# A LoRA kernel on one Trainium2 core: all of x held in SBUF, loads ahead of stores, groups of four tiles

## The chip, the core and the metric

The kernel runs on one core of one Trainium2 chip. The core has a matmul engine (PE, whose weight loads are listed apart as PEld), a vector engine (DVE), a scalar engine (ACT), GpSimd (POOL) and a sync engine (SP), which run their own instruction streams and meet at semaphores, and 16 DMA engines that carry data between the chip's memory (HBM) and the on-chip memory (SBUF, 128 partitions). PE writes to PSUM, a second on-chip memory. The metric is device time in microseconds of one execution; lower is better.

## The reference

```python
batch, seq, d_model, r = 16, 512, 768, 16
x: (16, 512, 768) float32;  A: (768, 16);  B: (16, 768);  scale = 0.5

def reference(x, A, B, scale):
    lora = np.matmul(np.matmul(x, A), B)
    return (x + scale * lora).astype(np.float32)
```

8192 tokens of 768 numbers go in and out: 25.2 MB each way. The two matmuls are thin (rank 16).

## The kernel before

**Tiles.** 128 tokens make a tile, 64 tiles in all; in SBUF a tile takes 768 floats in each of the 128 partitions. `PARTS` cuts the tiles into blocks of 8, 8, 16, 16 and 16. In a block of S tiles each partition holds S tokens that follow each other in memory, so that a load or a store moves one long run for each partition. `x_all` has room for `ROOM` = 48 tiles; the last block uses the places of tiles 0 to 15 again. The sum is written over x in place and stored from there.

**Groups.** The compute goes by groups of `GROUP` = 8 tiles, `NG` = 8 groups. Each group takes these steps:

- `narrowed`: ACT casts the first four tiles of x to half precision into `xn`, POOL the other four.
- `turned`: DVE transposes `xn` in blocks of 32 x 32 words into `xt`. A word is a pair of half-precision numbers, so the pair stays together.
- `projected`: PE multiplies `xt` by the block-diagonal `w_bd` (made from A in the start-up) in 24 matmuls that add up in `y_ps`; the moving side has 32 columns for each tile of the group, 256 here.
- ACT scales the four quarters of `y_ps` into the block-diagonal `y_bd` (four `e.mul`).
- `raised(p)`: for each pair of tiles PE multiplies `y_bd` by `b_mm` (B, spread over the partitions) into one of two PSUM buffers `lora`, four matmuls for a pair.
- `summed(g, p)` on DVE adds `lora` to the pair of x tiles in place.

There is one `xn`, one `xt`, one `y_bd`, one `y_ps`. `s_taken` tells that PE has begun to read a group's `xt` (so `xn` may be written again), `s_y` that its projection is done, `s_lora` counts raised pairs, `s_free` gives a PSUM buffer back, `s_sum` counts the blocks whose sums are complete.

**Order.** It is written out by hand for each engine. DVE transposes group g+1 ahead of group g's four sums. PE runs a loop over the groups: raise two pairs, half of the next projection, raise two pairs, the other half. SP issues every transfer on one queue: loads 0 to 5 at the start (A and B between them), then, when two groups are summed, stores 0 and 1; it waits until store 0 has landed and issues load 6 into its place, the same with store 1 and load 7, and then issues stores 2 to 4 as their sums are done. The function `summed(k)` in SP's part waits for `s_sum` and then also gives PE the last PSUM buffer of that group.

**Start-up.** POOL clears buffers, makes the selection matrix `pick`, casts B and builds `w_bd` from the transposed A; PE spreads B with `pick`; ACT copies it to `b_mm`.

Of the kernel before, what the change touches and what calls it, by code (L numbers as in the profile page):

```python
# [10 lines left out]

PARTS = [8, 8, 16, 16, 16]


GROUP = 8

SUB = 4

# [8 lines left out]
def kernel(  # L29
# [28 lines left out]
    def ps(name, shape):  # L58
        return nc.alloc_psum_tensor(name, shape, fp32).ap()

    ROOM = sum(PARTS[:-1])
    x_all = sb("x_sb", [P, ROOM, D], fp32)

    a_rows = sb("a_rows", [P, 64 * R], fp32)
    a_t = sb("a_t", [P, 2, R, Q], fp32)
    w_one = sb("w_one", [Q, NC, 2, R], MM_DT)
    b_rows = sb("b_rows", [P, D], fp32)  # L70
    b_half = sb("b_half", [P, D], MM_DT)
    pick = sb("pick", [P, NQ, Q], MM_DT)
    w_bd = sb("w_bd", [P, NC, 2, P], MM_DT)
    b_mm = sb("b_mm", [P, D], MM_DT)
    xn = sb("xn", [P, GROUP, D], MM_DT)
    xt = sb("xt", [P, GROUP, D], MM_DT)
    y_bd = sb("y_bd", [P, GROUP, P], MM_DT)
    lora = [ps(f"lora_ps{i}", [P, 2, D]) for i in range(2)]
    y_ps = ps("ps_yt", [P, GROUP, Q])

    sems = []

# [20 lines left out]
    def tiles(t, n):  # L103
        return x_all[:, ds(t % ROOM, n), :]

    LOADS = [
        (0, 0, 2), (0, 2, 6), (1, 0, 8), (2, 0, 8), (2, 8, 8), (3, 0, 16), (4, 0, 8), (4, 8, 8)
    ]
    s_load = [sem(f"s_load{k}") for k in range(len(LOADS))]

# [4 lines left out]
    assert SETS * SET == NC  # L115
    s_a, s_b = sem("s_a"), sem("s_b")
    s_ready, s_brows, s_pick = sem("s_ready"), sem("s_brows"), sem("s_pick")
    s_w, s_bh, s_bp, s_bm = sem("s_w"), sem("s_bh"), sem("s_bp"), sem("s_bm")
    s_first, s_narrow, s_turned, s_taken = sem("s_first"), sem("s_narrow"), sem("s_turned"), sem("s_taken")
    s_y, s_spread, s_lora = sem("s_y"), sem("s_spread"), sem("s_lora")  # L120

    s_free = [sem(f"s_free{p}") for p in range(PAIRS)]
    s_out0, s_out1, s_raise = sem("s_out0"), sem("s_out1"), sem("s_raise")

    s_sum, s_out = sem("s_sum"), sem("s_out")

    MMS = 2 * NC
    STORES = [(0, 0, 8), (1, 0, 8), (2, 0, 16), (3, 0, 16), (4, 0, 16)]

    STORED = [where.index((i, s + n - 1)) // GROUP for i, s, n in STORES]  # L130

# [3 lines left out]
    def on_sync(e):  # L135
        def load(k):
            ld = LOADS[k]
            e.dma_start(out=held(*ld), in_=memory(x2, *ld)).then_inc(s_load[k], 16)  # L138

        def summed(k):  # L140
            e.wait_ge(s_sum, k + 1)
            if STORED[k] + 1 < NG:

                e.sem_inc(s_free[PAIRS - 1], 1)

        def store(k, done):
            st = STORES[k]
            e.dma_start(out=memory(out2, *st), in_=held(*st)).then_inc(done, 16)

        load(0)  # L150
        load(1)
        e.wait_ge(s_ready, 1)
        blocks = A.rearrange("(c e) r -> c (e r)", e=64)
        for c in range(SETS):
            e.dma_start(
                out=a_rows[c : SET * SET : SET, :], in_=blocks[ds(c * SET, SET), :]
            ).then_inc(s_a, 16)
        e.wait_ge(s_brows, 1)
        e.dma_start(out=b_rows[0 : R * APART : APART, :], in_=B).then_inc(s_b, 16)
        for k in range(2, len(LOADS) - 2):  # L160
            load(k)

        for p in range(2, PAIRS):
            e.sem_inc(s_free[p], 1)
        summed(0)
        summed(1)


        e.wait_ge(s_lora, 2 * PAIRS + 2)
        store(0, s_out0)  # L170
        store(1, s_out1)
        e.wait_ge(s_out0, 16)
        load(len(LOADS) - 2)
        e.wait_ge(s_out1, 16)
        load(len(LOADS) - 1)
        for k in range(2, len(STORES)):
            summed(k)
            if k == 2:


                e.wait_ge(s_raise, 6)
            store(k, s_out)

    here = set()

    def narrowed(e, copy, g, first, n=SUB):
        t = g * GROUP + first
        for k in dict.fromkeys(load_of(t + k) for k in range(n)):
            if (e, k) not in here:
                here.add((e, k))  # L190
                e.wait_ge(s_load[k], 16)
        if g:
            e.wait_ge(s_taken, g)
        ins = copy(out=xn[:, ds(first, n), :], in_=tiles(t, n))  # L194

        ins.then_inc(s_narrow if g else s_first if first else s_a, 1)

    def on_gpsimd(e):
        e.memset(a_rows[0:Q], 0.0).then_inc(s_ready, 1)  # L199
        e.memset(b_rows, 0.0).then_inc(s_brows, 1)  # L200
        e.memset(pick, 0.0).then_inc(s_pick, 1)
        e.memset(w_bd.rearrange("p c k m -> p (c k m)").bitcast(fp32), 0.0)  # L202
        e.memset(y_bd.rearrange("p s m -> p (s m)").bitcast(fp32), 0.0).then_inc(s_ready, 1)  # L203
        e.wait_ge(s_pick, 1)
        e.affine_select(  # L205
            out=pick, in_=pick, compare_op=mybir.AluOpType.not_equal, fill=1.0, base=0,
            pattern=[[0, NQ], [-APART, Q]], channel_multiplier=1,
        ).then_inc(s_pick, 1)
        narrowed(e, e.tensor_copy, 0, 0, SUB // 2)
        e.wait_ge(s_pick, 2)  # L210
        e.wait_ge(s_b, 16)
        e.tensor_copy(out=b_half, in_=b_rows).then_inc(s_bh, 1)  # L212
# [6 lines left out]
        for b in range(NQ):  # L219
# [4 lines left out]
        for g in range(1, NG):  # L224
            narrowed(e, e.tensor_copy, g, SUB)

    def on_scalar(e):
        narrowed(e, e.copy, 0, SUB // 2, SUB // 2)
        narrowed(e, e.copy, 0, SUB)
        e.wait_ge(s_bp, 1)  # L230
        e.copy(out=b_mm, in_=lora[0][:, 0, :]).then_inc(s_bm, 1)  # L231
        for g in range(NG):
            if g + 1 < NG:
                narrowed(e, e.copy, g + 1, 0)
            e.wait_ge(s_y, g + 1)
            for b in range(NQ):
                q = ds(b * Q, Q)
                last = e.mul(out=y_bd[q, :, q], in_=y_ps[q, :, :], mul=sc)  # L238
            last.then_inc(s_spread, 1)

    def on_vector(e):
# [6 lines left out]
        def turned(first, n):  # L248
            ts = [v[:, ds(first, n), :].bitcast(fp32) for v in (xt, xn)]
            return e.transpose(out=ts[0], in_=ts[1])  # L250

        def summed(g, p):
            xs = tiles(g * GROUP + 2 * p, 2)
            e.wait_ge(s_lora, g * PAIRS + p + 1)
            ins = e.tensor_tensor(out=xs, in0=xs, in1=lora[p % 2], op=mybir.AluOpType.add)  # L255
            if p + 1 == PAIRS and g in STORED:
                ins.then_inc(s_sum, 1)
            elif g + 1 < NG or p + 2 < PAIRS:
                ins.then_inc(s_free[p], 1)

        for h in range(2):
            e.wait_ge(s_first, h + 1)
            ins = turned(h * SUB, SUB)
        ins.then_inc(s_turned, 1)
        for g in range(NG):
            if g + 1 < NG:
                e.wait_ge(s_y, g + 1)
                e.wait_ge(s_narrow, 2 * (g + 1))  # L268
                turned(0, GROUP).then_inc(s_turned, 1)
            for p in range(PAIRS):  # L270
                summed(g, p)

    def on_tensor(e):


        xv = xt.rearrange("p s (c j k) -> p s c j k", c=NC, k=2)

        def projected(first, last):
            for m in range(first, last):
                c, k = divmod(m, 2)  # L280
                mm = e.matmul(  # L281
                    y_ps, w_bd[:, c, k, :], xv[:, :, c, :, k],
                    start=(m == 0), stop=(m == MMS - 1),
                )
                if m == 0:
                    mm.then_inc(s_turned, -1)
# [6 lines left out]
        def raised(p):  # L293
            if p == 0:
                e.wait_ge(s_spread, 1)
            free = s_free[(p + 2) % PAIRS]
            e.wait_ge(free, 1)
            t = lora[p % 2]
            mms = []
            for k in range(2):  # L300
                for n0, w in ((0, 512), (512, 256)) if k == 0 else ((0, 256), (256, 512)):
                    mms.append(e.matmul(  # L302
                        t[:, k, ds(n0, w)], y_bd[:, 2 * p + k, :], b_mm[:, ds(n0, w)],
                        start=True, stop=True,
                    ))
            if p == 0:
                mms[0].then_inc(s_raise, 1)
# [9 lines left out]
                b_half[:, ds(n0, w)], start=True, stop=True,  # L317
            )
        last.then_inc(s_bp, 1)
        e.wait_ge(s_w, 1 + NQ)  # L320
        e.wait_ge(s_turned, 1)
        projected(0, MMS)
        e.wait_ge(s_bm, 1)
        with e.Fori(0, NG - 1):
            raised(0)
            raised(1)
            e.wait_ge(s_turned, 1)
            projected(0, MMS // 2)
            raised(2)
            raised(3)  # L330
            projected(MMS // 2, MMS)
        for p in range(PAIRS):
            raised(p)

    on_sync(nc.sync)
    on_gpsimd(nc.gpsimd)
# [6 lines left out]

    nc.gpsimd.wait_ge(s_sum, len(STORED))
    nc.gpsimd.sem_clear(range(nums[0], s_sum.num))
    nc.gpsimd.wait_ge(s_out, (len(STORES) - 2) * 16)
    nc.gpsimd.sem_clear(range(s_sum.num, s_out.num + 1))
    section.close()

# [34 lines left out]
```

## Time and profile before

| | |
|---|---|
| median of 3 runs | 123.55 us (123.46 to 123.61) |
| profiled execution: span, first to last instruction | 121.9 us |
| HBM read, written | 25.26 MB, 25.17 MB |
| mean rate over the span | 414 GB/s |
| DVE, PE, ACT, POOL busy | 81.7, 50.5, 37.4, 28.4 us |

The profile shows one execution. A row of a group reads: line, engine, operation, tile written <- tiles read, shapes, count | busy us in total, mean ns of one | idle time of that engine just before, and what ended it. A row in order of time begins with its start and duration in us; in square brackets stands how long the engine had been idle, and what released it. SPq is SP's sequencer, which issues DMAs. A stretch gives its start and end, its length, the busy time of each engine with the number of instructions, PEclk (the clock granted to PE, 1.00 is full speed), the busy share of the 16 DMA engines and the rate; a packet counts where it starts. The digits over 40 slices are tenths. Busy time of an engine is not yet a bound: which wait ends last decides.

### The profile page before, as it was taken

How to read it: one execution, taken by the hardware profiler on the slowest of the kernel's cores; microseconds unless marked ns; L12 is line 12 of the kernel's file. 1: busy time of each engine (PE TensorE's matmuls, PEld its weight loads, DVE VectorE, ACT ScalarE, POOL GpSimd, SP SyncE). 2: the span in 40 equal slices, each digit the busy share in tenths (PEclk: the TensorE clock that was granted, in tenths of full speed). 3: DMA queues.
4: the chain of work that ended last, by engine and by line, in shares of the span. 5: the costliest groups of instructions: out<-in, count | busy, mean ns of one | idle time of the engine just before them, and what ended most of it. 6: DMA issues, size and time to landing. Idle time of an engine off the chain costs nothing.

```text
span 121.9 us, 885 instructions
## 1 busy us (share of the span) xinstructions
PE 50.5 (41%) x322; PEld 29.3 (24%) x322; DVE 81.7 (67%) x42; ACT 37.4 (31%) x43; POOL 28.4 (23%) x24
## 2 busy tenths in 40 slices
PE   0000239487457457647756714774674320000000
PEld 0000026244233233424424402442442110000000
DVE  0003850799999999999999959999995991000000
ACT  4003929444426402917230093643004000000000
POOL 7732638044026002607100090630000000000000
PEclk9999999999999999999999999999999985555555
DMA  3999999999997996999989999998998999899890
GB/s 67 421 429 429 443 443 403 451 435 419 476 516 339 435 516 298 460 403 443 443 363 460 427 427 468 451 484 387 419 500 387 403 516 403 371 516 419 355 516 0
DMA packets 1928, 50.43 MB, mean 414 GB/s; under 512 B 236, under 2 KB 236, under 8 KB 392
## 3 DMA queue, kind: packets, MB, share of 16 engines
q1 hardware_dynamic: 1928, 50.43, 96.8%
HBM read 25.26 MB, written 25.17 MB: 414 GB/s over the span
## 4 chain that ended last, share of the span: by engine, by line
DVE 33%; DMA 29%; PE 9%; ACT 6%; POOL 2%; issue 2%; SPq 0%; DVEq 0%
DVE x_sb L255 21%; DMA x_sb<-in_x_dram 20%; DVE xt L250 12%; DMA out_dram<-x_sb 9%; PE ps_yt L281 6%; ACT xn L194 3%; PE lora_ps L302 3%; ACT y_bd L238 2%; POOL xn L194 2%; SPq L138 0%; SPq L379 0%; DVEq L268 0%; SPq L133 0%
## 5 line engine op out<-in xcount | busy, mean ns | idle before, releaser
L255 DVE TENSOR_TENSOR x_sb<-x_sb,lora_ps 128x1536 f32<-128x1536 f32 x32 | 53.7, 1735 | 1.4 <-PE lora_ps L302 1.4
L302 PE MATMUL lora_ps<-b_mm,y_bd 128*128 128x512 f16 (+1 forms) x128 | 25.1, 328 | 23.7 <-ACT y_bd L238 15.3
L194 ACT CAST xn<-x_sb 128x3072 f16<-128x3072 f32 (+1 forms) x9 | 23.4, 2609 | 37.2 <-DMA x_sb<-in_x_dram 28.0
L250 DVE STREAM_TRANSPOSE xt<-xn 128x3072 f32<-128x3072 f32 (+1 forms) x9 | 27.0, 3005 | 6.7 <-PE ps_yt L281 4.9
L194 POOL CAST xn<-x_sb 128x3072 f16<-128x3072 f32 (+1 forms) x8 | 20.7, 2588 | 45.3 <-DMA x_sb<-in_x_dram 28.6
L281 PE MATMUL ps_yt<-xt,w_bd 128*128 128x256 f16 x192 | 25.7, 285 | 11.9 <-DVE xt L250 11.9
L281 PEld LDWEIGHTS ps_yt<-xt,w_bd 128*128 128x128 f16 x192 | 18.7, 100 | 19.6 <-issue 15.0
L302 PEld LDWEIGHTS lora_ps<-b_mm,y_bd 128*128 128x128 f16 x128 | 10.5, 97 | 36.8 <-ACT y_bd L238 17.5
L238 ACT ACTIVATE y_bd<-ps_yt 32x256 f16<-32x256 f32 x32 | 12.0, 374 | 17.7 <-PE ps_yt L281 17.4
L243 DVE STREAM_TRANSPOSE a_t<-a_rows 32x1024 f32<-32x1024 f32 x1 | 1.9, 1945 | 11.2 <-DMA a_rows<-in_A_dram 11.2
L315 PE MATMUL lora_ps<-b_half,pick 128*128 128x512 f16 (+1 forms) x2 | 0.8, 500 | 12.5 <-POOL b_half L212 12.5
L315 PEld LDWEIGHTS lora_ps<-b_half,pick 128*128 128x128 f16 x2 | 0.1, 105 | 12.5 <-issue 12.5
L220 POOL COPY w_bd<-w_one 32x384 f16<-32x384 f16 x4 | 2.0, 501 | 0.2
L212 POOL CAST b_half<-b_rows 128x768 f16<-128x768 f32 x1 | 0.8, 830 | 4.5 <-DMA b_rows<-in_B_dram 4.5
L194 ACT ACT_TABLE_LOAD x1 | 1.3, 1283 | 0.9 <-SPq L133 0.9
L202 POOL MEMSET w_bd<- 128x1536 f32 x1 | 1.4, 1372 | 0.0
L199 POOL MEMSET a_rows<- 32x1024 f32 x1 | 0.9, 941 | 0.5 <-SPq L133 0.5
L214 POOL CAST w_one<-a_t 32x384 f16<-32x384 f32 x1 | 0.8, 847 | 0.9 <-DVE a_t L243 0.9
L231 ACT CAST b_mm<-lora_ps 128x768 f16<-128x768 f32 x1 | 0.8, 798 | 0.0
L200 POOL MEMSET b_rows<- 128x768 f32 x1 | 0.7, 727 | 0.0
L203 POOL MEMSET y_bd<- 128x512 f32 x1 | 0.5, 514 | 0.0
L205 POOL TENSOR_SCALAR_AFFINE_SELECT pick<-pick 128x128 f16<-128x128 f16 x1 | 0.3, 300 | 0.0
(5 smaller groups left out, 0.6 us busy)
## 6 DMA issues: line engine op xcount, KB each, us to landing
out_dram<-x_sb SPq DMA_DIRECT2D x3, 6144.0 KB, 20.0
x_sb<-in_x_dram SPq DMA_DIRECT2D x5, 3072.0 KB, 14.8
x_sb<-in_x_dram SPq DMA_DIRECT2D x1, 6144.0 KB, 41.9
out_dram<-x_sb SPq DMA_DIRECT2D x2, 3072.0 KB, 14.9
x_sb<-in_x_dram SPq DMA_DIRECT2D x1, 2304.0 KB, 9.7
x_sb<-in_x_dram SPq DMA_DIRECT2D x1, 768.0 KB, 4.5
a_rows<-in_A_dram SPq DMA_DIRECT2D x3, 16.0 KB
b_rows<-in_B_dram SPq DMA_DIRECT2D x1, 48.0 KB, 7.4
```

The source lines that it names most:

```text
L194: ins = copy(out=xn[:, ds(first, n), :], in_=tiles(t, n))
L199: e.memset(a_rows[0:Q], 0.0).then_inc(s_ready, 1)
L202: e.memset(w_bd.rearrange("p c k m -> p (c k m)").bitcast(fp32), 0.0)
L212: e.tensor_copy(out=b_half, in_=b_rows).then_inc(s_bh, 1)
L220: e.tensor_copy(out=w_bd[ds(b * Q, Q), :, :, ds(b * Q, R)], in_=w_one).then_inc(s_w, 1)
L238: last = e.mul(out=y_bd[q, :, q], in_=y_ps[q, :, :], mul=sc)
L243: e.transpose(out=a_t[0:Q].rearrange("i k r c -> i (k r) c"), in_=a_rows[0:Q].rearrange("c (i k r) -> c (k r) i", k=2, r=R),).then_inc(s_r ...
L250: return e.transpose(out=ts[0], in_=ts[1])
L255: ins = e.tensor_tensor(out=xs, in0=xs, in1=lora[p % 2], op=mybir.AluOpType.add)
L281: mm = e.matmul(y_ps, w_bd[:, c, k, :], xv[:, :, c, :, k], start=(m == 0), stop=(m == MMS - 1),)
L302: mms.append(e.matmul(t[:, k, ds(n0, w)], y_bd[:, 2 * p + k, :], b_mm[:, ds(n0, w)], start=True, stop=True,))
L315: last = e.matmul(lora[0][:, 0, ds(n0, w)], pick.rearrange("p b r -> p (b r)"), b_half[:, ds(n0, w)], start=True, stop=True,)
```

## The change

- `x_all` has room for all 64 tiles; the blocks are 8, 16, 16, 12 and 12. There are still eight loads and five stores: loads of 2, 6, 8, 8, 16, 12, 10 and 2 tiles, stores of whole blocks.
- SP issues loads 0 to 5 at the start, load 6 after the first raised pair, load 7 after the projection of group 7, then waits for load 6 to land and issues stores 0 and 1, and stores 2 to 4 as their sums are done.
- A group has 4 tiles, 16 groups. A projection's matmuls have 128 columns, a group has two pairs. `y_bd`, `y_ps` and the semaphores `s_turned` and `s_free` are doubled and go by even and odd groups. PE projects two groups ahead, in one piece after the raising of a group; DVE transposes group g+2 ahead of group g's two sums.
- The start-up's scratch (`a_rows`, `a_t`, `b_rows`, `b_half`, `pick`, `w_one`) and group 1's `xn` and `xt` lie in the part of `x_all` that load 6 fills.
- There is no `xt` of its own any more. Groups 0 and 2 to 7 are turned into the place of the last two tiles (which load 7 fills), groups 8 to 10 in place in `xn`, groups 11 to 15 into the place of tiles 0 and 1, after store 0 has landed. While a group is turned in place, the next cast waits for its projection (`s_y`) and not only for `s_taken`.
- DVE instead of POOL writes the last of the four copies of `w_bd`.
- PE's loop becomes two loops (three and two rounds of two groups) with groups written out between and behind them.

```diff
-PARTS = [8, 8, 16, 16, 16]
-GROUP = 8
-SUB = 4
+PARTS = [8, 16, 16, 12, 12]
+GROUP = 4
+SUB = 2
+PLACE = range(8, 11)
...
-    ROOM = sum(PARTS[:-1])
+    ROOM = sum(PARTS)
...
-    xt = sb("xt", [P, GROUP, D], MM_DT)
-    y_bd = sb("y_bd", [P, GROUP, P], MM_DT)
+    y_bd = sb("y_bd", [P, 2, GROUP, P], MM_DT)
-    y_ps = ps("ps_yt", [P, GROUP, Q])
+    y_ps = [ps(f"ps_yt{i}", [P, GROUP, Q]) for i in range(2)]
+    late = x_all[:, ds(ROOM - PARTS[-1], PARTS[-1]), :].rearrange("p s d -> p (s d)")
...
+    xt_a, xt_c = turned_in(ROOM - SUB), turned_in(0)
+    def narrow_of(g):
+        return xn_1 if g == 1 else xn
+    def turn_of(g):
+        return xt_1 if g == 1 else xt_a if g < PLACE[0] else xn if g in PLACE else xt_c
...
     LOADS = [
-        (0, 0, 2), (0, 2, 6), (1, 0, 8), (2, 0, 8), (2, 8, 8), (3, 0, 16), (4, 0, 8), (4, 8, 8)
+        (0, 0, 2), (0, 2, 6), (1, 0, 8), (1, 8, 8), (2, 0, 16), (3, 0, 12), (4, 0, 10), (4, 10, 2)
     ]
...
-    STORES = [(0, 0, 8), (1, 0, 8), (2, 0, 16), (3, 0, 16), (4, 0, 16)]
+    STORES = [(i, 0, S) for i, S in enumerate(PARTS)]
...
-        for p in range(2, PAIRS):
-            e.sem_inc(s_free[p], 1)
+        for p in range(PAIRS):
+            e.sem_inc(s_free[1][p], 1)
+        e.wait_ge(s_lora, 1)
+        load(len(LOADS) - 2)
         summed(0)
         summed(1)
-        e.wait_ge(s_lora, 2 * PAIRS + 2)
+        e.wait_ge(s_y, PLACE[0])
+        load(len(LOADS) - 1)
+        e.wait_ge(s_load[len(LOADS) - 2], 16)
         store(0, s_out0)
-        store(1, s_out1)
-        e.wait_ge(s_out0, 16)
-        load(len(LOADS) - 2)
-        e.wait_ge(s_out1, 16)
-        load(len(LOADS) - 1)
+        store(1, s_out)
         for k in range(2, len(STORES)):
             summed(k)
-            if k == 2:
-                e.wait_ge(s_raise, 6)
             store(k, s_out)
...
-        if g:
-            e.wait_ge(s_taken, g)
+        if g - 1 in PLACE:
+            e.wait_ge(s_y, g)
+        elif g > 1:
+            e.wait_ge(s_taken, g if g > 2 else 1)
...
         for g in range(NG):
-            if g + 1 < NG:
-                e.wait_ge(s_y, g + 1)
+            if g + 2 < NG:
+                if g + 2 == PLACE[-1] + 1:
+                    e.wait_ge(s_out0, 16)
+                elif g + 2 not in PLACE:
+                    e.wait_ge(s_y, g + 2 if g else 1)
                 e.wait_ge(s_narrow, 2 * (g + 1))
-                turned(0, GROUP).then_inc(s_turned, 1)
+                turned(g + 2)
             for p in range(PAIRS):
                 summed(g, p)
...
-        with e.Fori(0, NG - 1):
-            raised(0)
-            raised(1)
-            e.wait_ge(s_turned, 1)
-            projected(0, MMS // 2)
-            raised(2)
-            raised(3)
-            projected(MMS // 2, MMS)
-        for p in range(PAIRS):
-            raised(p)
+        def step(g):
+            for p in range(PAIRS):
+                raised(g % 2, p)
+            if g + 2 < NG:
+                projected(g % 2, turn_of(g + 2))
```

More of the change, by code (lines that the diff above doesn't have):

```diff
@@ L59, in ps @@
         return nc.alloc_psum_tensor(name, shape, fp32).ap()
-    ROOM = sum(PARTS[:-1])
+    ROOM = sum(PARTS)
     x_all = sb("x_sb", [P, ROOM, D], fp32)
[L67 to L72, printed above, removed]
     w_bd = sb("w_bd", [P, NC, 2, P], MM_DT)
@@ L75, with lent, turned_in @@
     xn = sb("xn", [P, GROUP, D], MM_DT)
-    xt = sb("xt", [P, GROUP, D], MM_DT)
-    y_bd = sb("y_bd", [P, GROUP, P], MM_DT)
+    y_bd = sb("y_bd", [P, 2, GROUP, P], MM_DT)
     lora = [ps(f"lora_ps{i}", [P, 2, D]) for i in range(2)]
-    y_ps = ps("ps_yt", [P, GROUP, Q])
+    y_ps = [ps(f"ps_yt{i}", [P, GROUP, Q]) for i in range(2)]
+    late = x_all[:, ds(ROOM - PARTS[-1], PARTS[-1]), :].rearrange("p s d -> p (s d)")
+    taken = [0]
+    def lent(n, dtype=fp32):
+        n = n if dtype is fp32 else n // 2
+        taken[0], first = taken[0] + n, taken[0]
+        assert taken[0] <= (PARTS[-1] - SUB) * D
+        v = late[:, ds(first, n)]
+        return v if dtype is fp32 else v.bitcast(dtype)
+    a_rows = lent(64 * R)
+    a_t = lent(2 * R * Q).rearrange("p (k r c) -> p k r c", k=2, r=R)
+    b_rows = lent(D)
+    b_half = lent(D, MM_DT)
+    pick = lent(P, MM_DT).rearrange("p (b r) -> p b r", b=NQ)
+    w_one = lent(NC * 2 * R, MM_DT)[0:Q].rearrange("i (c k r) -> i c k r", c=NC, k=2)
+    xn_1 = lent(GROUP * D, MM_DT).rearrange("p (s d) -> p s d", s=GROUP)
+    xt_1 = lent(GROUP * D, MM_DT).rearrange("p (s d) -> p s d", s=GROUP)
+    def turned_in(t):
+        v = x_all[:, ds(t, SUB), :].rearrange("p s d -> p (s d)").bitcast(MM_DT)
+        return v.rearrange("p (s d) -> p s d", s=GROUP)
+    xt_a, xt_c = turned_in(ROOM - SUB), turned_in(0)
[3 more added lines that the diff above has]
+        return xt_1 if g == 1 else xt_a if g < PLACE[0] else xn if g in PLACE else xt_c
     sems = []
@@ L117 @@
     s_ready, s_brows, s_pick = sem("s_ready"), sem("s_brows"), sem("s_pick")
+    s_wv = sem("s_wv")
     s_w, s_bh, s_bp, s_bm = sem("s_w"), sem("s_bh"), sem("s_bp"), sem("s_bm")
-    s_first, s_narrow, s_turned, s_taken = sem("s_first"), sem("s_narrow"), sem("s_turned"), sem("s_taken")
+    s_first, s_narrow, s_taken = sem("s_first"), sem("s_narrow"), sem("s_taken")
+    s_turned = [sem(f"s_turned{h}") for h in range(2)]
     s_y, s_spread, s_lora = sem("s_y"), sem("s_spread"), sem("s_lora")
-    s_free = [sem(f"s_free{p}") for p in range(PAIRS)]
-    s_out0, s_out1, s_raise = sem("s_out0"), sem("s_out1"), sem("s_raise")
+    s_free = [[sem(f"s_free{h}_{p}") for p in range(PAIRS)] for h in range(2)]
+    s_out0 = sem("s_out0")
     s_sum, s_out = sem("s_sum"), sem("s_out")
     MMS = 2 * NC
-    STORES = [(0, 0, 8), (1, 0, 8), (2, 0, 16), (3, 0, 16), (4, 0, 16)]
+    STORES = [(i, 0, S) for i, S in enumerate(PARTS)]
     STORED = [where.index((i, s + n - 1)) // GROUP for i, s, n in STORES]
@@ L142, in summed @@
             if STORED[k] + 1 < NG:
-                e.sem_inc(s_free[PAIRS - 1], 1)
+                e.sem_inc(s_free[STORED[k] % 2][PAIRS - 1], 1)
         def store(k, done):
@@ L191, in narrowed @@
                 e.wait_ge(s_load[k], 16)
-        if g:
-            e.wait_ge(s_taken, g)
-        ins = copy(out=xn[:, ds(first, n), :], in_=tiles(t, n))
-        ins.then_inc(s_narrow if g else s_first if first else s_a, 1)
+        if g - 1 in PLACE:
+            e.wait_ge(s_y, g)
+        elif g > 1:
+            e.wait_ge(s_taken, g if g > 2 else 1)
+        ins = copy(out=narrow_of(g)[:, ds(first, n), :], in_=tiles(t, n))
+        ins.then_inc(s_narrow if g > 1 else s_first if g or first else s_a, 1)
     def on_gpsimd(e):
@@ L202, in on_gpsimd @@
         e.memset(w_bd.rearrange("p c k m -> p (c k m)").bitcast(fp32), 0.0)
-        e.memset(y_bd.rearrange("p s m -> p (s m)").bitcast(fp32), 0.0).then_inc(s_ready, 1)
+        e.memset(y_bd.rearrange("p h s m -> p (h s m)").bitcast(fp32), 0.0).then_inc(s_ready, 1)
         e.wait_ge(s_pick, 1)
@@ L208, in on_gpsimd @@
         ).then_inc(s_pick, 1)
-        narrowed(e, e.tensor_copy, 0, 0, SUB // 2)
+        narrowed(e, e.tensor_copy, 0, 0)
         e.wait_ge(s_pick, 2)
@@ L218, in on_gpsimd @@
         e.wait_ge(s_w, 1)
-        for b in range(NQ):
+        for b in range(NQ - 1):
             e.tensor_copy(
@@ L223, in on_gpsimd @@
             e.wait_ge(s_w, b + 2)
-        for g in range(1, NG):
+        for g in range(2, NG):
             narrowed(e, e.tensor_copy, g, SUB)
     def on_scalar(e):
-        narrowed(e, e.copy, 0, SUB // 2, SUB // 2)
         narrowed(e, e.copy, 0, SUB)
+        narrowed(e, e.copy, 1, 0, GROUP)
         e.wait_ge(s_bp, 1)
         e.copy(out=b_mm, in_=lora[0][:, 0, :]).then_inc(s_bm, 1)
+        narrowed(e, e.copy, 2, 0)
         for g in range(NG):
-            if g + 1 < NG:
-                narrowed(e, e.copy, g + 1, 0)
             e.wait_ge(s_y, g + 1)
@@ L237, in on_scalar @@
                 q = ds(b * Q, Q)
-                last = e.mul(out=y_bd[q, :, q], in_=y_ps[q, :, :], mul=sc)
+                last = e.mul(out=y_bd[q, g % 2, :, q], in_=y_ps[g % 2][q, :, :], mul=sc)
             last.then_inc(s_spread, 1)
+            if 1 <= g < NG - 2:
+                narrowed(e, e.copy, g + 2, 0)
     def on_vector(e):
@@ L246, in on_vector, with turned @@
         ).then_inc(s_ready, 1)
-        def turned(first, n):
-            ts = [v[:, ds(first, n), :].bitcast(fp32) for v in (xt, xn)]
-            return e.transpose(out=ts[0], in_=ts[1])
+        def turned(g):
+            ts = [v.bitcast(fp32) for v in (turn_of(g), narrow_of(g))]
+            e.transpose(out=ts[0], in_=ts[1]).then_inc(s_turned[g % 2], 1)
         def summed(g, p):
@@ L257, in summed @@
                 ins.then_inc(s_sum, 1)
[L258 to L264, printed above, removed]
-        for g in range(NG):
-            if g + 1 < NG:
-                e.wait_ge(s_y, g + 1)
+            elif g + 1 < NG:
+                ins.then_inc(s_free[g % 2][p], 1)
+        for g in range(2):
+            e.wait_ge(s_first, g + 1)
+            turned(g)
+            if g == 0:
+                b = NQ - 1
+                e.wait_ge(s_w, 1)
+                e.tensor_copy(
+                    out=w_bd[ds(b * Q, Q), :, :, ds(b * Q, R)], in_=w_one
+                ).then_inc(s_wv, 1)
+        for g in range(NG):
+            if g + 2 < NG:
[3 more added lines that the diff above has]
+                    e.wait_ge(s_y, g + 2 if g else 1)
                 e.wait_ge(s_narrow, 2 * (g + 1))
-                turned(0, GROUP).then_inc(s_turned, 1)
+                turned(g + 2)
             for p in range(PAIRS):
@@ L273, in on_tensor, with projected @@
     def on_tensor(e):
-        xv = xt.rearrange("p s (c j k) -> p s c j k", c=NC, k=2)
-        def projected(first, last):
-            for m in range(first, last):
+        def projected(h, xt):
+            xv = xt.rearrange("p s (c j k) -> p s c j k", c=NC, k=2)
+            e.wait_ge(s_turned[h], 1)
+            for m in range(MMS):
                 c, k = divmod(m, 2)
                 mm = e.matmul(
-                    y_ps, w_bd[:, c, k, :], xv[:, :, c, :, k],
+                    y_ps[h], w_bd[:, c, k, :], xv[:, :, c, :, k],
                     start=(m == 0), stop=(m == MMS - 1),
@@ L285, in projected @@
                 if m == 0:
-                    mm.then_inc(s_turned, -1)
+                    mm.then_inc(s_turned[h], -1)
                 if m == 1:
@@ L291, in projected, with raised @@
                     mm.then_inc(s_y, 1)
-        def raised(p):
+        def raised(h, p):
             if p == 0:
                 e.wait_ge(s_spread, 1)
-            free = s_free[(p + 2) % PAIRS]
+            free = s_free[1 - h][p]
             e.wait_ge(free, 1)
@@ L302, in raised @@
                     mms.append(e.matmul(
-                        t[:, k, ds(n0, w)], y_bd[:, 2 * p + k, :], b_mm[:, ds(n0, w)],
+                        t[:, k, ds(n0, w)], y_bd[:, h, 2 * p + k, :], b_mm[:, ds(n0, w)],
                         start=True, stop=True,
@@ L319, in on_tensor @@
         last.then_inc(s_bp, 1)
-        e.wait_ge(s_w, 1 + NQ)
-        e.wait_ge(s_turned, 1)
-        projected(0, MMS)
+        e.wait_ge(s_w, NQ)
+        e.wait_ge(s_wv, 1)
+        projected(0, turn_of(0))
+        projected(1, turn_of(1))
         e.wait_ge(s_bm, 1)
-        with e.Fori(0, NG - 1):
-            raised(0)
-            raised(1)
-            e.wait_ge(s_turned, 1)
-            projected(0, MMS // 2)
-            raised(2)
-            raised(3)
-            projected(MMS // 2, MMS)
-        for p in range(PAIRS):
-            raised(p)
+        def step(g):
[3 more added lines that the diff above has]
+                projected(g % 2, turn_of(g + 2))
+        g = 0
+        while g < NG:
+            n = 1
+            while g + 2 * n + 3 < NG and all(
+                turn_of(t + 2) is turn_of(g + 2) for t in range(g, g + 2 * n + 2)
+            ):
+                n += 1
+            same = g + 3 < NG and turn_of(g + 2) is turn_of(g + 3)
+            if same and n > 1 and g % 2 == 0:
+                with e.Fori(0, n):
+                    step(g)
+                    step(g + 1)
+                g += 2 * n
+            else:
+                step(g)
+                g += 1
     on_sync(nc.sync)
@@ L345 @@
     nc.gpsimd.sem_clear(range(nums[0], s_sum.num))
-    nc.gpsimd.wait_ge(s_out, (len(STORES) - 2) * 16)
+    nc.gpsimd.wait_ge(s_out, (len(STORES) - 1) * 16)
     nc.gpsimd.sem_clear(range(s_sum.num, s_out.num + 1))
```

1 line of the change is left out of this document (removed).

## The prediction

> **What bounds the kernel now.** I read the page from the top: the shares of the engines, the slices, the queue, the groups with each shape apart, then the chip's work in order of time, and last the DMA traffic stretch by stretch.
>
> ```profile
> span 121.9 us, 885 instructions
> PE 50.5 (41%) x322; PEld 29.3 (24%) x322; DVE 81.7 (67%) x42; ACT 37.4 (31%) x43; POOL 28.4 (23%) x24
> PEclk9999999999999999999999999999999985555555
> DMA  3999999999997996999989999998998999899890
> q1 hardware_dynamic: 1928, 50.43, 96.8%
> ...
> DVE 33%; DMA 29%; PE 9%; ACT 6%; POOL 2%; issue 2%; SPq 0%; DVEq 0%
> ```
>
> Two rows seem to disagree. The chain puts 33% on DVE, but it goes back through whatever released the last store, and that store was put into a queue that was still full. The queue row decides: the 16 DMA engines are busy 96.8% of the span, from the second slice to the last but one, while DVE does nothing in the last quarter. Every byte must be moved once in and once out, so only what keeps this queue from running full can change the time. I follow it by its landings.
>
> ```profile
> 0.97 0.85 SPq L138 DMA_DIRECT2D x_sb<-in_x_dram  x2
> ...
> 17.18 4.76 PE L281 MATMUL ps_yt<-xt,w_bd 128*128 128x256 f16 x24 [3.90 <-DVE xt L250]
> ...
> 18.57 2.75 ACT L194 CAST xn<-x_sb 128x3072 f16<-128x3072 f32 x1 [2.52 <-DMA x_sb<-in_x_dram]
> ...
> 25.51 1.49 PE L281 MATMUL ps_yt<-xt,w_bd 128*128 128x256 f16 x12 [0.46 <-DVE xt L250]
> ...
> 27.06 0.82 PE L302 MATMUL lora_ps<-b_mm,y_bd 128*128 128x512 f16 x4
> ...
> 48.02 2.75 ACT L194 CAST xn<-x_sb 128x3072 f16<-128x3072 f32 x1 [5.66 <-DMA x_sb<-in_x_dram]
> ...
> 55.30 0.34 SPq L138 DMA_DIRECT2D x_sb<-in_x_dram  x1
> ...
> 62.70 0.34 SPq L138 DMA_DIRECT2D x_sb<-in_x_dram  x1
> ...
> 70.08 2.75 ACT L194 CAST xn<-x_sb 128x3072 f16<-128x3072 f32 x1 [7.88 <-DMA x_sb<-in_x_dram]
> ...
> 77.40 2.75 ACT L194 CAST xn<-x_sb 128x3072 f16<-128x3072 f32 x1 [3.01 <-DMA x_sb<-in_x_dram]
> ```
>
> From 18.57 on, each wait for DMA here, and each issue by SP, ended when a transfer had landed: at 18.57 load 2 (tiles 8 to 15), at 48.02 load 5, at 55.30 and 62.70 stores 0 and 1 (SP waits for each before it issues a load), at 70.08 and 77.40 loads 6 and 7. Per tile of 128 tokens (393 KB) that is (48.02 - 18.57) / 32 = 0.920 us, then for 8 tiles each 7.28, 7.40, 7.38 and 7.32 us: 0.910, 0.925, 0.923, 0.915. The best, 0.910, I call the pace of a full queue. After 77.40 come 48 tiles of stores, 48 x 0.910 = 43.7, and 121.9 - 77.40 - 43.7 = 0.8 us of tail.
>
> At that pace the queue from 18.57 would need 112 x 0.910 = 101.9 (48 tiles to load, 64 to store), plus 0.8: 121.3. So at most 0.6 us can be had behind the start-up. Where it is lost shows in the stretches:
>
> ```profile
> core 0: us, PE busy (x) PEld busy (x) DVE busy (x) ACT busy (x) POOL busy (x), PEclk, DMA share, GB/s
> 46.00:48.00 2.00, 1.66 (x12) 0.79 (x9) 2.00 (x2) 0.00 (x0) 0.00 (x0) 1.00 0.72 307
> ...
> 60.00:62.00 2.00, 0.63 (x6) 0.30 (x4) 2.00 (x3) 1.30 (x4) 0.00 (x0) 1.00 0.94 356
> ...
> 76.00:78.00 2.00, 1.50 (x12) 1.08 (x12) 2.00 (x3) 0.60 (x1) 0.57 (x1) 1.00 1.20 516
> ```
>
> A packet is counted where it starts, so single stretches jump; still, the low ones stand where the queue goes from loads to stores (46 to 48: 29.45 - 32 x 0.910 = 0.33 us lost up to 48.02) and back to loads (60 to 62: 0.12 and 0.10 in the two transfers around it). The next turn to stores, at 77, cost 0.04 in its transfer and shows no low stretch.
>
> **The change part by part.** *Order of transfers.* Before: loads of 48 tiles, stores of 16, loads of 16, stores of 48: three turns. After: 64 in, 64 out, one turn, in 13 transfers as before. The instruction order of the built kernel has all eight loads ahead of the stores on SP. Loads 0 to 2 and those of A and B are the same, so 18.57 stays. Load 6 now waits for group 0's first raising, near 22, under a queue that has work until 18.57 + 36 x 0.910 = 51.3. Then tiles 16 to 61 take 46 x 0.910 = 41.9, to 60.4. Load 7 (two tiles) takes 2 x 0.910 = 1.8, to 62.3. The turn to stores costs between 0.04 and 0.33 by the two of its kind above; I take 0.15, a little under the middle, since what the slower DMA engines still have in hand there is a two-tile load, the smallest of all. That is 62.45. Stores: 64 x 0.910 = 58.2, to 120.7. Tail 0.8: 121.5.
>
> *The new wait in the middle.* SP stands at load 6's semaphore before it issues store 0, and every later store queues behind it, and so does SP's release of a stored group's last PSUM half to PE; the first group concerned, group 9, isn't summed before 75 (below), so PE doesn't wait for it. Late next would be the first store packet. It needs load 6's landing, an issue and the way to the first packet. The nearest row is the first load of all:
>
> ```profile
> 0.00:2.00 2.00, 0.00 (x0) 0.00 (x0) 0.00 (x0) 1.09 (x1) 1.25 (x6) 1.00 0.02 3
> ...
> x_sb<-in_x_dram SPq DMA_DIRECT2D x1, 768.0 KB, 4.5
> ```
>
> Issued at 0.97, its first packets start just before 2.00: 1.0 us. All that is not pace in it is 4.5 - 1.8 = 2.7, on an empty queue, with the first packets themselves slow. So from the last byte of load 6 to the first store packet lie 1.0 (if the landing is seen at once) to 2.7 us, and load 7 covers 1.8 of them: a gap of 0 to 0.9. I take 0, nearer the lower end, since the 4.5 holds the slow start as well; the upper end is a rival below. Were load 7 not queued in time, the whole 1.0 to 2.7 would show. The Trainium skill (DMA: Bandwidth & Descriptors, section on the anatomy of one DMA) puts set-up and completion at about 2.0 us for any transfer, which speaks against this step: by it the gap would be 2.0 - 1.8 = 0.2 us and the sum 121.7.
>
> *Compute, which must only keep ahead of the queue.* The groups go from 8 tiles to 4.
>
> ```profile
> L255 DVE TENSOR_TENSOR x_sb<-x_sb,lora_ps 128x1536 f32<-128x1536 f32 x32 | 53.7, 1735 | 1.4 <-PE lora_ps L302 1.4
> L194 ACT CAST xn<-x_sb 128x1536 f16<-128x1536 f32 x1 | 1.5, 1472 | 8.9 <-DMA x_sb<-in_x_dram 8.9
> L250 DVE STREAM_TRANSPOSE xt<-xn 128x1536 f32<-128x1536 f32 x2 | 3.5, 1751 | 0.4 <-ACT xn L194 0.4
> L238 ACT ACTIVATE y_bd<-ps_yt 32x256 f16<-32x256 f32 x32 | 12.0, 374 | 17.7 <-PE ps_yt L281 17.4
> ```
>
> DVE per group: one transpose of the half size, 1.75, and two sums at 53.7 / 32 = 1.68: 5.1 us, 16 groups. ACT: one cast 1.47 and four small multiplies, at most 4 x 0.37: 3.0. POOL casts the other half, beside ACT. PE: two pairs of raising matmuls at 0.82, and 24 projecting ones of 128 columns. Those aren't in the trace; the 256-column form takes 1.49 / 12 = 0.124 once running, so 24 lie between half of that, 1.5, and all of it, 3.0. I take 3.0, the row itself, which weighs against the change: PE 4.6 of 5.1 us. DVE sets the pace.
>
> Group 2's cast can start at 18.57, so its transpose starts at about 20.1. The waits from there: 0.6 while the pipeline fills (group 0's sums need its raising, which comes after four multiplies on ACT, 1.5 behind that cast, and 0.82 on PE: 22.4, against the transpose's end at 21.85); 0.8 at group 6, whose tiles come with the 16-tile load 4, landed at 18.57 + 24 x 0.910 = 40.4 and cast by 41.9, against 20.1 + 0.6 + 4 x 5.1 = 41.1. Then the three groups turned in place: a cast waits until the projection before it has read xn, so after each transpose come 3.0 + 1.47 and about 0.2 of hand-over, against two sums, 3.36, that cover it: 1.3 each, 3.9 for three (with projections of 1.5 us, 0). Group 11's transpose is then due at 20.1 + 1.4 + 9 x 5.1 = 67.4 to 71.3; it also waits for store 0, landed at 62.45 + 8 x 0.910 = 69.7. So it starts between 69.8 and 71.3, and behind it on DVE stand the sums that stores 2 to 4 wait for. They end at +1.75 + 3.36 (group 9), +3 x 5.1 more (group 12) and, with 5 transposes and 14 sums in all, 32.3 (group 15): at the latest 76.4, 91.7 and 103.6.
>
> What the queue needs: stores 2, 3 and 4 issued 1.0 before the queue is empty, at 62.45 plus 24, 40 and 52 tiles: 83.3, 97.9 and 108.8. Load 7 must be issued before 60.4; group 7's projection, which it waits for, ends by 20.1 + 1.4 + 5 x 5.1 + 1.75 + 3.0 = 51.8. The margins are 6.9, 6.2, 5.2 and 8.6 us. They hide all of it: A's and B's scratch moved into x_sb, the doubled y_bd and PSUM y, the last w_bd copy on DVE instead of POOL, the waits above. With that cover gone, each us beyond it is one at the end.
>
> The span goes from 121.9 to 121.5, by -0.4. The median of the runs, 123.55, stands 1.65 over the span; so **123.15**.
>
> **The rivals.**
> (1) *The middle wait shows.* The gap of up to 0.9 us opens on all 16 queues. For it: 2.7 us in the one short load of the trace. Against it: 1.0 to the first packet. With 0.3 to 0.9 more the time is 123.45 to 124.05: no change or slightly slower.
> (2) *PE becomes the bound: slower.* Shorter bursts could leave PE's clock low. For it: the first projection ran 24 matmuls in 4.76, 0.198 each against 0.124 later, and the row of granted clocks has 5 at the end, when PE goes idle. Against it: the stretches above have a granted clock of 1.00 with PE busy between 0.63 and 1.66 of 2 us, and PE would be as full after. At that price a pair of raising matmuls takes 0.82 x 0.198 / 0.124 = 1.3 and a group of PE 2 x 1.3 + 3.0 = 5.6 (a projection of half the columns at half the clock costs 3.0 again). The two first groups' projections end near 17.18 + 4.76 = 21.9 (as many columns as the one of 24 x 256); from there PE decides if a group takes over (108.8 - 21.9) / 16 = 5.4. At 5.6 the last sums end at 111.5, and 1.0 + 12 x 0.910 + 0.8 later the span: 124.2, in the runs 125.9.
> (3) *PE waits for its code: slower.* What is one short loop on PE becomes two loops and four groups written out between them, 322 matmuls where 82 stood. For the price of a fetch behind a full queue the nearest row is B's load, a small transfer:
>
> ```profile
> b_rows<-in_B_dram SPq DMA_DIRECT2D x1, 48.0 KB, 7.4
> ```
>
> Between 0 and 7.4 us each. With one, 7.4 - 5.2 = 2.2 is not hidden, 125.4; with two 132.8. Against it: no second queue moves anything in the span, though PE's loop ran seven times. The Trainium skill (Runtime: NRT & Kernel Launch, section on instruction fetch) says that a sequencer streams its code ahead while it runs, but that a taken branch to a page that it doesn't hold forces a fetch; no run here shows one.
>
> **How the numbers follow.** Forecast 0.58, rival (1) 0.25, (2) 0.11, (3) 0.06. The forecast's own range is its turn and pace, 122.85 to 123.4. The range 122.8 to 125.0 takes in (1) and leaves out most of (2) and (3). A measurement tells about 0.2%, 0.25 us, from no change: faster means under 123.3, which is 0.50 of the forecast's 0.58; the rest, 0.08, and 0.17 of (1) are no change; 0.08 of (1), (2) and (3) are slower: 0.25.
>
> **What would show it.** Right: DMA share 97% or more, load 7 issued near 52, one low stretch near 62 at most, store 0 issued near 60.9, stores 2 to 4 issued before 83, 98 and 109, DVE done by 105. A slice of DMA below 8 near 62 is rival (1). PEclk of 0.5 inside the span, or DVE idle behind PE's L338, is (2); a gap on PE that nothing explains, or a second queue, is (3). The forecast fails if the pace per tile changes when only one direction runs.

## The result, and the profile after

The changed kernel takes 125.8 us (125.75 to 125.95) against 123.53 of before in the same runs: a ratio of 1.018 (95% interval 1.0165 to 1.0193). It is slower by 2.3 us, where -0.4 was forecast. The page of after, the lines that answer to those of before:

```profile
span 124.0 us, 1339 instructions
PE 55.5 (45%) x514; PEld 36.5 (29%) x514; DVE 82.8 (67%) x50; ACT 43.9 (35%) x82; POOL 29.2 (24%) x30
PEclk9999999999999955999999985999999998555555
DMA  3999999999899899899699999699799999999980
q1 hardware_dynamic: 1928, 50.43, 95.4%
q8 instruction: 2, 0.03, 0.1%
q14 instruction: 2, 0.02, 0.0%
```

The queue is full as before, a little less (95.4% against 96.8%), and there are two queues that before did not have: they carry instructions, two pieces of 16 KB (q8) and two of 8 KB (q14). In order of time, after:

```profile
18.62 1.47 ACT L221 CAST xn<-x_sb 128x1536 f16<-128x1536 f32 x1 [2.48 <-DMA x_sb<-in_x_dram]
...
41.62 1.47 ACT L221 CAST xn<-x_sb 128x1536 f16<-128x1536 f32 x1 [6.44 <-DMA x_sb<-in_x_dram]
...
45.15 2.72 PE L317 MATMUL ps_yt<-x_sb,w_bd 128*128 128x128 f16 x24 [3.86 <-DVE x_sb L278]
...
50.14 1.54 PE L317 MATMUL ps_yt<-x_sb,w_bd 128*128 128x128 f16 x24
...
58.23 1.78 DVE L278 STREAM_TRANSPOSE xn<-xn 128x1536 f32<-128x1536 f32 x1
...
61.65 0.35 SPq L179 DMA_DIRECT2D out_dram<-x_sb  x1
...
63.33 1.78 DVE L278 STREAM_TRANSPOSE xn<-xn 128x1536 f32<-128x1536 f32 x1
...
71.04 1.78 DVE L278 STREAM_TRANSPOSE x_sb<-xn 128x1536 f32<-128x1536 f32 x1 [2.63 <-DMA out_dram<-x_sb]
...
92.69 10.04 DVE L283 TENSOR_TENSOR x_sb<-x_sb,lora_ps 128x1536 f32<-128x1536 f32 x6
```

Load 2 lands at 18.6 as forecast. Load 4 lands at 41.6 where 40.4 was forecast: 1.2 late. Nothing more is lost up to load 6 (61.65, forecast 60.4) or much up to store 0 (71.04, forecast 69.7); the other half of the 2.5 us of span comes later. The DMA queues of two stretches, and of the very end, show what lies there. From 18.6 to 41.6:

```profile
q1 hardware_dynamic: 297, 10.04, 101.4%
q8 instruction: 1, 0.02, 0.3%
```

From 71 to 87:

```profile
q1 hardware_dynamic: 159, 7.03, 102.4%
q8 instruction: 1, 0.02, 0.4%
```

From 120.9 to the end at 124.0:

```profile
DMA packets 9, 0.04 MB, mean 12 GB/s; under 512 B 8, under 2 KB 8, under 8 KB 8
q1 hardware_dynamic: 9, 0.04, 2.9%
```

One instruction packet lies in each of the two stretches in which time goes missing. 0.4% of 16 engines over 16 us is about 1.0 us of one engine. At the end, eight of the nine packets have 4 bytes each and carry no data; the ninth, 0.04 MB, is the one run of data that starts after 120.9. So a single DMA engine has data to start when the other 15 have none left: the kernel ends with its slowest DMA engine.

The trace says the same more directly. A transfer of x has 16 such small packets and 16 landing marks (steps of its semaphore), as many as there are DMA engines; whoever waits for it goes on with the last mark. Of load 4's marks 15 stand by 40.45, where 40.4 was forecast; the last comes at 41.60. One mark stays 1.15 behind the other 15 at loads 5, 6 and 7 too. The 16 KB pieces start at 32.3, before load 4 lands, and at 77.8, before store 1 lands, and there one mark is 1.3 behind again.

Theory F, after this: PE's longer code is fetched in pages over the same 16 DMA engines as the data, and the engine that fetches a page is late from there on. Its rival T: the loss belongs to the new order (SP's wait between loads and stores, one direction at a time, the small groups).

### The profile page after: what moved, and what is told of

The parts are those of the page before. It is cut to its first block, busy times and chain, and to the rows that moved or that the text cites. A ratio compares the mean times of both kernels' runs of the same rounds, so it can differ in the third digit from the quotient of the medians.

```text
span 124.0 us, 1339 instructions
## 1 busy us (share of the span) xinstructions
PE 55.5 (45%) x514; PEld 36.5 (29%) x514; DVE 82.8 (67%) x50; ACT 43.9 (35%) x82; POOL 29.2 (24%) x30
## 3 DMA queue, kind: packets, MB, share of 16 engines
q1 hardware_dynamic: 1928, 50.43, 95.4%
## 4 chain that ended last, share of the span: by engine, by line
DMA 51%; DVE 22%; issue 4%; SPq 2%; ACT 2%; POOL 1%; PE 1%; POOLq 0%
DMA x_sb<-in_x_dram 43%; DVE x_sb L283 15%; DMA out_dram<-x_sb 8%; DVE x_sb L278 7%; SPq L186 2%; ACT xn L221 1%; ACT y_bd L264 1%; POOL x_sb L226 1%; PE lora_ps L338 1%; SPq L190 0%; POOLq L429 0%; SPq L164 0%
## 5 line engine op out<-in xcount | busy, mean ns | idle before, releaser
L221 ACT CAST xn<-x_sb 128x1536 f16<-128x1536 f32 x15 | 22.1, 1472 | 45.0 <-PE ps_yt L317 27.1
L221 POOL CAST xn<-x_sb 128x1536 f16<-128x1536 f32 x15 | 22.0, 1466 | 54.1 <-PE ps_yt L317 43.0
L317 PE MATMUL ps_yt<-x_sb,w_bd 128*128 128x128 f16 x312 | 23.1, 237 | 16.4 <-DVE x_sb L278 13.8
L317 PEld LDWEIGHTS ps_yt<-x_sb,w_bd 128*128 128x128 f16 x312 | 21.3, 105 | 20.8 <-issue 20.6
L278 DVE STREAM_TRANSPOSE x_sb<-xn 128x1536 f32<-128x1536 f32 x12 | 21.2, 1763 | 8.6 <-PE ps_yt L317 3.1
L264 ACT ACTIVATE y_bd<-ps_yt 32x128 f16<-32x128 f32 x64 | 17.2, 268 | 5.8 <-PE ps_yt L317 4.9
L317 PE MATMUL ps_yt<-xn,w_bd 128*128 128x128 f16 x72 | 4.6, 218 | 3.0 <-DVE xn L278 3.0
L317 PEld LDWEIGHTS ps_yt<-xn,w_bd 128*128 128x128 f16 x72 | 4.2, 96 | 4.0 <-issue 4.0
L278 DVE STREAM_TRANSPOSE xn<-xn 128x1536 f32<-128x1536 f32 x3 | 5.3, 1772 | 0.0
L221 ACT CAST x_sb<-x_sb 128x3072 f16<-128x3072 f32 x1 | 2.7, 2746 | 0.0
```

What stands on the lines that cost most here:

```text
L221: ins = copy(out=narrow_of(g)[:, ds(first, n), :], in_=tiles(t, n))
L264: last = e.mul(out=y_bd[q, g % 2, :, q], in_=y_ps[g % 2][q, :, :], mul=sc)
L278: e.transpose(out=ts[0], in_=ts[1]).then_inc(s_turned[g % 2], 1)
L317: mm = e.matmul(y_ps[h], w_bd[:, c, k, :], xv[:, :, c, :, k], start=(m == 0), stop=(m == MMS - 1),)
```

## The experiments

**All groups in place: less PE code, the same order.** In the changed kernel

```diff
-PLACE = range(8, 11)
+PLACE = range(2, 16)
-        store(0, s_out0)
+        store(0, s_out)
-    nc.gpsimd.wait_ge(s_out, (len(STORES) - 1) * 16)
+    nc.gpsimd.wait_ge(s_out, len(STORES) * 16)
```

> Groups 2 to 15 are all turned in place in xn, so PE's loop is one loop again: 130 matmuls written instead of 322 (about 285 PE instructions instead of 685; before has 82 and 184). The order of transfers and the wait between loads and stores stay as in the changed kernel. Theory F (each 16 KB page of PE's code that has to be fetched runs over one of the 16 DMA engines amid the data, puts that one about 1.2 us behind, and the end waits for the slowest): one page at most is left, 0 to 1 fetches instead of 2, so 123.1 (none) to 124.4 (one). Theory T (the loss comes from the turn: SP's wait for load 6, or stores only, or the 4-tile groups): 125.8 as the changed kernel, since all of that is still there.

Measured: 125.17 us, 1.0131 of before (1.0114 to 1.0147), one 16 KB fetch (and one of 8 KB) instead of two (and two):

```profile
q8 instruction: 1, 0.02, 0.1%
```

It comes down by 0.6, which lies between the two: T said nothing at all, F 1.4. It is 0.8 above F's 124.4. About half of that is F's base, since the new order without a PE fetch measures 123.53 below and not 123.1; the rest stays open.

**The same with more code.** The loop has six rounds, the last four groups are written out.

```diff
-            while g + 2 * n + 3 < NG and all(
+            while n < 6 and g + 2 * n + 3 < NG and all(
```

> As the one before, but the loop has six rounds instead of seven and the last four groups are written out: 194 matmuls, about 417 PE instructions. What is computed, and every transfer, is the same as in the run before. F: one fetch of PE code, 124.3 to 124.5, and at least as long as the run before. T: the same time as the run before.

Measured: 125.28 us, 1.0129 (1.0112 to 1.0146), again one fetch of 16 KB. With 417 PE instructions instead of 285 the number of fetches is the same and so is the time, which fits fetches that count and not instructions. F's figure, 124.3 to 124.5, is missed as in the run before. T said the same time as well, so the run tells nothing between the two.

**The kernel before with PE's loop written out.**

```diff
-        with e.Fori(0, NG - 1):
+        for _ in range(NG - 1):
```

> The kernel before with nothing changed but that PE's loop over seven groups is written out: 322 matmuls, about 672 PE instructions, as many as in the changed kernel. F: two fetches on a second queue and one DMA engine about 2.4 us behind: 124.7 to 126.0. T: 123.5, since its order of transfers is the old one.

Measured: 124.76 us, 1.0098 (1.0071 to 1.0124). Its queues, and in order of time its waits for loads 5 and 6:

```profile
q1 hardware_dynamic: 1928, 50.43, 96.2%
q8 instruction: 2, 0.03, 0.1%
```

```profile
49.43 2.75 ACT L194 CAST xn<-x_sb 128x3072 f16<-128x3072 f32 x1 [6.98 <-DMA x_sb<-in_x_dram]
...
71.26 2.75 ACT L194 CAST xn<-x_sb 128x3072 f16<-128x3072 f32 x1 [8.47 <-DMA x_sb<-in_x_dram]
```

Load 5 lands at 49.43 where before had 48.02, load 6 at 71.26 instead of 70.08. No transfer and no step of the compute was changed; the written-out loop alone costs 1.2 us. T can't say that. F holds at its lower end: the delays of two fetches don't simply add here (1.4 at load 5, 1.0 at the end of the span). At load 5 one landing mark is 1.5 behind the other 15; at load 7, behind the second fetch, two are late (78.03 and 78.52, the other 14 by 77.18). So two engines are late there, where one fetch had made one late.

**The changed kernel with everything written out** (PE 1073 instructions):

```diff
-            if same and n > 1 and g % 2 == 0:
+            if False:
```

> The changed kernel with both of PE's loops written out: 514 matmuls, about 1073 PE instructions. F: three or four fetches instead of two, 127.0 to 128.2. T: 125.8.

Measured: 126.09 us, 1.0205 (1.0188 to 1.0222), four fetches of 16 KB:

```profile
q8 instruction: 4, 0.07, 0.2%
```

The direction is F's, the size isn't: two more fetches cost 0.3, which the intervals hardly tell from nothing, and not 1.2 to 2.4.

**The new order without a PE fetch.** On top of the first kernel:

```diff
-    MMS = 2 * NC
+    MMS = NC
-                c, k = divmod(m, 2)
+                c, k = m, 0
```

> As e1_all_in_place, but each projection runs 12 matmuls instead of 24 (the odd half of every chunk of x @ A is left out of the computation), which brings PE's code to about 189 instructions, next to the 184 of before. All transfers and waits stay. PE isn't the bound here, so its shorter work alone should give nothing. Theory F (code fetches): no second queue in the span, and the forecast's sum for the new order holds at last: 123.0 to 123.5, and 1.6 to 2.0 us less than e1_all_in_place. Theory T (the turn, the stores alone, or the small groups): 125.0 to 125.3, as e1_all_in_place.

Measured: 123.53 us, 1.0001 of before (0.9991 to 1.0011), 1.64 less than with one fetch. Its page; in order of time, its wait for load 4 and the issue of store 0; and the least, median and greatest time from issue to landing of its five stores:

```profile
span 121.7 us, 947 instructions
q1 hardware_dynamic: 1928, 50.43, 96.9%
q14 instruction: 1, 0.01, 0.0%
```

```profile
40.55 1.47 ACT L221 CAST xn<-x_sb 128x1536 f16<-128x1536 f32 x1 [3.41 <-DMA x_sb<-in_x_dram]
...
60.57 0.82 SPq L179 DMA_DIRECT2D out_dram<-x_sb  x2
```

```profile
DMA to landing us min/median/max: 9.3/22.8/26.8
```

No 16 KB piece is left; one of 8 KB is, so F's "no second queue" is met for PE's code only. With no PE fetch the forecast's path comes out: load 4 at 40.5 (40.4), load 6 at 60.57 (60.4), store 0 at 60.57 + 9.3 = 69.9 (69.7), the span 121.7 (121.5). The order of transfers costs nothing against before, and brings nothing that the interval shows.

**Is it PE's shorter work or its shorter code?** The kernel above with PE's loop written out (the line of the run with everything written out).

> As e5_in_place_half_projection (12 matmuls a projection, the odd half of each chunk left out), with PE's loop written out: 322 matmuls, the number of the changed kernel, about 670 PE instructions. Every engine executes the same work in the same order as in e5. Theory F: two fetches of PE's code, 125.0 to 125.9. The other reading of e5 (theory P: e5 was faster because PE did half the projection, not because its code was short): 123.5, as e5.

Measured: 125.82 us, 1.0172 (1.0145 to 1.0198): the time of the changed kernel, with half the projection. Two 16 KB fetches are back; its queues, and its issue of store 0:

```profile
q8 instruction: 2, 0.03, 0.1%
q14 instruction: 1, 0.01, 0.0%
```

```profile
61.69 0.82 SPq L179 DMA_DIRECT2D out_dram<-x_sb  x2
```

Load 6 lands 1.1 later than in the kernel above. Theory P falls: with the same work in the same order, the longer code alone makes the 2.3 us. T falls too, since order, wait and groups are those of the 123.53.

**The middle wait.** Both without this line: the kernel with half the projection, and the changed kernel.

```diff
-        e.wait_ge(s_load[len(LOADS) - 2], 16)
```

> As the run before, without SP's wait for load 6 ahead of store 0 (the stores then stand in the queue right behind load 7). The price of the middle wait where no DMA engine is behind: by my step 0 (load 7 covers it), so the same time within 0.2 us; by the first rival 0.3 to 0.9 us less.

> The changed kernel without SP's wait for load 6. By F the DMA engine that fetched the code sets the end and never stood idle at the turn (it was still busy with load 7 when the first store packets came), so 125.5 to 125.9, no or nearly no gain, though the other 15 engines finish about 0.8 us earlier. By T or the first rival (the wait holds all 16 up): 124.9 or less.

Measured: without a fetch 124.37 us, 1.0068 (1.0048 to 1.0088), that is 0.84 *slower* than with the wait; with two fetches 125.17, 1.0128 (1.0105 to 1.0151), 0.6 faster. Both readings missed the first one; the second lies between F's 125.5 and T's 124.9. The stretch of the turn where no PE code is fetched, without the wait and then with it (start and end, length, engines, PEclk, DMA share, GB/s):

```profile
60.00:62.00 2.00, 0.81 (x4) 0.32 (x4) 2.00 (x3) 1.95 (x4) 1.30 (x1) 1.00 0.97 319
```

```profile
60.00:62.00 2.00, 0.81 (x4) 0.32 (x4) 2.00 (x2) 1.95 (x4) 1.41 (x1) 1.00 1.19 493
```

Single stretches jump, but over the six us from 58 to 64 the DMA engines are as busy without the wait (mean share 0.98 against 0.97) and start less (364 against 407 GB/s). By the trace it is the small load that slows down: load 7's 128 packets, 6 KB each, take 0.32 us on average without the wait and 0.24 with it, while store 0's take 0.91 and 0.92. That is 0.7 us on each of the 16 engines, most of the 0.84. The wait keeps loads and stores apart, at the price that all engines stand until the last one has loaded. That this price is higher than the saving when one engine is 1.2 us late fits the 0.6 gained.

**Another engine's code.** The kernel before, and behind POOL's last cast

```diff
+        for k in range(256):
+            e.memset(idle[:, ds(k, 1)], 0.0)
```

> The kernel before with 256 memsets of one element each behind POOL's last cast (some 0.1 us each, so POOL is done by about 107, well ahead of the last landing at 121); PE's code is the short one. Is it PE's code or any engine's? By F in its wide form, POOL's code (about 310 instructions instead of 53) is fetched over the same DMA engines too: a second queue in the span and 123.8 to 124.8. If only PE's code counts: no such queue and 123.5.

Measured: 124.2 us, 1.0053 (1.0034 to 1.0072).

```profile
q14 instruction: 2, 0.02, 0.0%
```

POOL's row in order of time shows that it stood still inside its memsets:

```profile
87.06 3.32 POOL L228 MEMSET idle<- 128x1 f32 x99 [1.91 <-issue]
```

POOL's code comes in pieces of 8 KB on the other instruction queue (the first at 85.4, just where POOL stands), and two of them cost 0.6 us. Up to 85.4 the landings are as early as in the kernel before; at store 2 two marks are about 1 us behind the other 14 (92.28 and 92.66, against 91.34), and two are at the end. The memsets are done by 90.4 and all but two of the marks are in time, which speaks for the fetches and against the memsets' own work. So it isn't PE's code alone that can do this; ACT, DVE and SP were not tried. The small q14 pieces of the changed kernel may be code of another engine than PE; no run shows of which.

## Why the prediction was wrong

*The pace of a full queue (0.910 us a tile), the turn (0.15), the new wait (0).* Right for the path: the kernel without PE fetches follows it to 0.2 us in each landing. There the first store packet starts 0.9 after load 6 has landed (61.43 against 60.56), before load 7's last packet does (61.73): load 7 covers the wait, as the step said. From load 7's landing, 62.41, to store 0's, 69.91, are 7.50, so turn and wait cost 0.2 over the 7.28 of eight tiles. The Trainium skill's 2.0 us for a transfer (DMA: Bandwidth & Descriptors, section on the anatomy of one DMA, whose heading names transfers that GpSimd issues; here SP issues them) makes an estimated 0.15 + 0.2 = 0.35 of it; the trace, 0.2, is nearer the forecast's 0.15. What the step did not see is that the wait saves time: without it the kernel isn't equally fast but 0.84 slower.

*The offset of 1.65 us to the runs.* Mis-sized. In the runs shown with the results before has spans from 121.5 to 122.0 and times 1.8 above them; the profiled execution, 121.9, was one of the longer ones. The forecast's 121.5 stood for 123.3, a gain of 0.2 at the edge of what can be told, and the new order without PE's fetches measures as no change.

*Compute keeps ahead.* Right, with room. 24 projecting matmuls of 128 columns take 1.54 once PE's clock is up, the lower of the two bounds (I took the upper one). The groups turned in place cost 0.1 each, not 1.3: 58.23 to 63.33 is 5.1 us against some 5.0 of the others. The last sum ends at 102.7, within the forecast's 102 to 104.

*Rival (2), PE's clock.* The clock does fall, twice inside the work, each time near a stretch in which PE idles some 3.8 us (before the row at 45.15, which takes 2.72 for 24 instead of 1.54, and before one at 72.97). The sums still end in time, so it costs nothing.

*Rival (3), the code.* This is where the failing step lies. I saw the loop of 82 matmuls become 322 written ones, but asked only what PE would lose by waiting for its code, and hid that behind PE's margin. But PE didn't wait: around the two fetches it idles at most 1.1 us at a time, released by DVE or SP, and the sums were in time (above). The fetch takes a DMA engine, and the terms "46 x 0.910" and "64 x 0.910" of the sum had no room for anything else on the one queue that sets the end. The evidence that I put against it, that no second queue moves anything in the span, was a fact of the short code. The sign it named, a second queue, did come. Measured for the term, which the sum put at nothing: +1.2 at load 4, as much again behind store 0, 2.3 us in all.

*The numbers.* The 125.8 lay outside the range of 122.8 to 125.0. 125.9 stood in rival (2) and 125.4 in rival (3), but for causes that the trace doesn't show, PE's clock and PE's wait for one fetch, so that they come near is luck. One reading was off, and nothing rests on it: DVE is idle in the last sixth of the span of before (its last sum ends at 101.0 of 121.9), not in the last quarter.

*Why the fetches don't add evenly.* Over the 123.53 without a PE fetch, one costs 1.6 (the first kernel), two 2.3, four 2.6; in the kernel before two cost 1.2. The landing marks show most of it. In the changed kernel one mark is late up to the middle wait; behind it all are later, since SP lets no engine store before the late one has loaded (median of store 0's marks 70.29, against 69.28 without a fetch). The second fetch then puts one engine behind the others again, and the last mark of the last store comes at 123.05 instead of 120.83. So across the wait the delays add. With everything written out, two of load 6's marks are 1.2 late side by side (61.74 and 61.81, the other 14 by 60.55), and two again at the end: two engines that are late at the same time cost hardly more than one.

Open: why one fetch costs 1.6, when its mark is only 0.85 late at load 4. That before's order with three turns and the new one with one come out the same was measured, but the new order was run without a PE fetch only with half the projection left out. No version here beats the kernel before.

## What to carry to other kernels

In a kernel whose DMA queue is full from end to end, everything that uses a DMA engine is on the path, code as well: count the instructions that each engine's program has as written, not as executed, and keep the loops rolled if written-out code brings fetches into the span. Look at the list of queues before and after a change, since one late DMA engine of 16 sets the end and hardly shows in a mean share (95.4% against 96.8%). And when a price is found for a rival, ask which resource it would take, not only which engine would wait.

## What was not expected of the hardware

A fetch of 16 KB of code takes about 1.0 us of one DMA engine and puts that engine's next landing 0.85 to 1.5 us behind the others. One appeared with 285 and 417 PE instructions and none with 184 or 189, two with 672 to 689 and four with 1073. Stores put right behind a small load without a wait slow the load's packets down (0.32 us instead of 0.24): 0.84 us for one turn.
